# A residual block on one core: the gate and up products as one block of 1024 columns, with seven tile products in place of eight for half of the k-tiles

## The chip, the core and the metric

The kernel runs on one core of one Trainium2 chip. The metric is device time in microseconds (us) from the first to the last instruction with what lies around them; lower is better. TensorE (PE in the profile) multiplies a stationary block by a moving block, loads the stationary block with an instruction of its own (PEld), and writes sums into eight banks of PSUM, each 128 x 512 float32. VectorE (DVE) and ScalarE (ACT) read PSUM and work on tiles in SBUF. GpSimd (POOL) and SyncE (SP) mostly start transfers here. Each engine takes its instructions in the order written for it and waits at the head of its queue until what the instruction needs is there.

## The reference

One layer of a hybrid block on 256 tokens of width 2048: sparse attention and a state-space mixer in parallel, gated and projected, then a channel mixer and a final norm. The change is in the channel mixer and in what feeds it:

```python
h = h + hybrid_mixer(u, ...)                  # its last product is merged @ w_out
u2 = rms_norm(h, g_ffn[i])
gate, up = jnp.split(u2 @ w_ffn_in[i], 2, axis=-1)      # 2048 -> 2 x 5632
h = h + (jax.nn.silu(gate) * up) @ w_ffn_out[i]         # 5632 -> 2048
return rms_norm(h, g_final)
```

All of it is float32.

## The kernel before, in words

The 256 tokens are two token tiles (t = 0, 1) of 128. The width 2048 is 16 k-tiles of 128. A product of float32 operands is made from three products of a reduced float32 format: every operand is split into a high part `hi` and a rest `lo`, and the kernel adds hi x hi, hi x lo and lo x hi (L149 to L151). So one tile product (128 tokens x 128 k x 512 columns) is three TensorE instructions, and its two operands have to be split first.

For the weights this happens as they arrive. `gemm` (L140) loads four k-tiles of one block of 512 columns as one transfer of 1 MB into `raw` (three buffers), and splits them in two halves of 128 x 1024: ScalarE writes `hi` (L181), VectorE `lo` (L182). `hi` and `lo` have four buffers each, and a buffer is free again once the last product that reads it is done. A half serves 2 k-tiles x 2 token tiles x 3 = 12 products.

The channel mixer takes 512 gate columns and the 512 up columns that belong to them as one of 11 pairs (`pair`, L696). Before: one `gemm` of 16 k-tiles for gate (96 products), one for up (96), silu on ScalarE (L700), one product of the two on VectorE (L703), then eight transposes on TensorE (L212) and the split into `act` (L199, L200). After five pairs the first half of the down projection follows (`w_f2`, L717), then six more pairs and the second half.

The stationary operand is h, transposed and scaled by the gain, as `h_hi` and `h_lo`, made by `trans_split` (L205) after each of the four blocks of the output projection `w_o` (L671 to L684). The products of PSUM have four banks (`mm`), transposes two, the rest two.

The order on each engine's queue is set when the program is built, by a scheduler with priorities; loads and splits of weights carry a high one (`tc.high_priority(PRE)`). The chip only follows that order.

## Time and profile before

| what | value |
|---|---|
| median of 3 runs | 1996.29 us (1995.64 to 2485.34) |
| span of the profiled execution | 1993.2 us |
| median less span | 3.1 us |
| TensorE | 1981.7 us busy (99%), 9230 products and transposes |
| VectorE | 1247.3 us busy (63%) |
| ScalarE | 979.0 us busy (49%) |
| read from HBM | 372.02 MB, 188 GB/s over the span |

The profile's page gives for the profiled execution its span, 1993.2 us, and no time of its own; the runs' median lies 3.1 us above it, and that is the part around the span that is used below. A TensorE row's duration covers the whole pipeline, so consecutive rows overlap; what a product costs is the distance between two starts. "idle before, releaser" in a row says how long the engine had been idle ahead of the instruction and what ended that.

### The profile page before, as it was taken

The page shows a single profiled execution, that of the slowest core. Times are in us where ns is not written, and L with a number is a line of the kernel's source. Part 1 is how long each engine was busy: PE and PEld are TensorE (multiplying, and loading weights), DVE is VectorE, ACT ScalarE, POOL GpSimd, SP SyncE. Part 2 cuts the span into 40 slices and gives each one's busy share as a digit, 9 for nine tenths or more (in the row PEclk, how much of TensorE's full clock was granted, in tenths as well). Part 3 has the DMA queues.
Part 4 walks back from the last instruction along what each step waited for, and adds up shares of the span by engine and source line. Part 5 has one row for each costly group of instructions (what it writes and reads, how often), then busy time and mean ns, then how long its engine had stood idle before and what let it go on. Part 6 is the DMA issues. An engine that isn't in the chain of part 4 may idle for free.

```text
span 1993.2 us, 23301 instructions
## 1 busy us (share of the span) xinstructions
PE 1981.7 (99%) x9230; PEld 1644.7 (83%) x9230; DVE 1247.3 (63%) x1665; ACT 979.0 (49%) x1161; POOL 37.0 (2%) x87
## 2 busy tenths in 40 slices
...
GB/s 279 225 162 177 190 190 169 203 198 174 191 206 169 181 163 204 170 169 169 190 172 197 181 200 201 190 190 190 180 193 197 211 190 191 190 189 191 189 192 127
DMA packets 54429, 375.69 MB, mean 188 GB/s; under 512 B 6304, under 2 KB 6816, under 8 KB 10672
## 3 DMA queue, kind: packets, MB, share of 16 engines
...
HBM read 372.02 MB, written 2.16 MB: 188 GB/s over the span
## 4 chain that ended last, share of the span: by engine, by line
PE 98%; issue 1%; DMA 0%; DVE 0%; SPq 0%; ACT 0%; POOLq 0%; POOL 0%; DVEq 0%; ACTq 0%
PE mm L149 31%; PE mm L151 31%; PE mm L150 31%; PE yp L501 1%; PE tr L212 1%; PE tr L415 1%; PE lg L603 1%; PE tr L524 0%; PE tr L478 0%; DMA raw<-in_w_a_dram 0%; PE tr L626 0%; PE tr L569 0%; PE tr L456 0%; PE sd L391 0%; PE sd L393 0%
## 5 line engine op out<-in xcount | busy, mean ns | idle before, releaser
L182 DVE TENSOR_TENSOR lo<-raw,hi 128x1024 fp32r<-128x1024 f32 (+2 forms) x689 | 834.7, 1213 | 641.4 <-ACT hi L181 638.4
L181 ACT ACTIVATE hi<-raw 128x1024 fp32r<-128x1024 f32 (+2 forms) x689 | 723.7, 1052 | 884.0 <-PE mm L151 818.6
L150 PE MATMUL mm<-lo,uh 128*128 128x512 f32 (+2 forms) x1184 | 461.0, 389 | 0.0
L151 PE MATMUL mm<-hi,ul 128*128 128x512 f32 (+2 forms) x1184 | 458.2, 388 | 0.2 <-DVE ul L203 0.2
L149 PE MATMUL mm<-hi,uh 128*128 128x512 f32 (+2 forms) x1184 | 452.9, 389 | 1.2 <-ACT hi L181 1.2
L149 PE MATMUL mm<-hi,hh 128*128 128x512 f32 x704 | 274.8, 390 | 0.0
L151 PE MATMUL mm<-hi,hl 128*128 128x512 f32 x704 | 274.7, 390 | 0.0
L150 PE MATMUL mm<-lo,hh 128*128 128x512 f32 x704 | 274.0, 389 | 0.0
L149 PEld LDWEIGHTS mm<-hi,uh 128*128 128x128 f32 x1184 | 222.3, 188 | 44.9 <-ACT hi L181 2.1
L151 PEld LDWEIGHTS mm<-hi,ul 128*128 128x128 f32 x1184 | 222.6, 188 | 42.4 <-DVE ul L203 0.5
L150 PEld LDWEIGHTS mm<-lo,uh 128*128 128x128 f32 x1184 | 222.7, 188 | 41.3 <-DVE lo L182 0.4
L150 PEld LDWEIGHTS mm<-lo,hh 128*128 128x128 f32 x704 | 132.2, 188 | 27.2
L151 PEld LDWEIGHTS mm<-hi,hl 128*128 128x128 f32 x704 | 132.2, 188 | 27.1
L149 PEld LDWEIGHTS mm<-hi,hh 128*128 128x128 f32 x704 | 132.2, 188 | 26.7
L149 PE MATMUL mm<-hi,act 128*128 128x512 f32 x352 | 137.1, 390 | 0.0
L151 PE MATMUL mm<-hi,act 128*128 128x512 f32 x352 | 137.1, 390 | 0.0
L150 PE MATMUL mm<-lo,act 128*128 128x512 f32 x352 | 136.9, 389 | 0.0
L151 PE MATMUL mm<-hi,yl 128*128 128x512 f32 x256 | 100.4, 392 | 0.0
L150 PE MATMUL mm<-lo,yh 128*128 128x512 f32 x256 | 100.4, 392 | 0.0
L149 PE MATMUL mm<-hi,yh 128*128 128x512 f32 x256 | 100.2, 395 | 0.0
L149 PEld LDWEIGHTS mm<-hi,act 128*128 128x128 f32 x352 | 66.1, 188 | 13.7
L150 PEld LDWEIGHTS mm<-lo,act 128*128 128x128 f32 x352 | 66.1, 188 | 13.6
...
## 6 DMA issues: line engine op xcount, KB each, us to landing
raw<-in_w_f_dram SPq DMA_DIRECT2D x132, 1024.0 KB, 4.8
raw<-in_w_m_dram SPq DMA_DIRECT2D x104, 1024.0 KB, 4.8
raw<-in_w_sb_dram SPq DMA_DIRECT2D x32, 1024.0 KB, 4.8
raw<-in_w_g_dram SPq DMA_DIRECT2D x32, 1024.0 KB, 4.8
raw<-in_w_ab_dram SPq DMA_DIRECT2D x16, 1024.0 KB, 4.8
raw<-in_w_o_dram SPq DMA_DIRECT2D x16, 1024.0 KB, 4.8
abc<-acum_d POOLq DMA_DIRECT2D x8, 1024.0 KB, 5.0
...
```

What stands on the lines that cost most here:

```text
L149: nc.tensor.matmul(o, lh, rh, start=(kt == 0), stop=False)
L150: nc.tensor.matmul(o, lh, rl, start=False, stop=False)
L151: nc.tensor.matmul(o, ll, rh, start=False, stop=(kt == nk - 1))
L181: hi_ops.append(nc.scalar.activation(hi[:, o], src[:, o], AF.Copy))
L182: nc.vector.tensor_tensor(lo[:, o], src[:, o], hi[:, o].bitcast(F32), ALU.subtract)
L212: nc.tensor.transpose(tp[:, c, t * P : (t + 1) * P], src(t, o), ident)
L415: nc.tensor.transpose(tp[:, c, t * P : (t + 1) * P], xk[:, t, o : o + P], ident)
L501: nc.tensor.matmul(yp[64 * c : 64 * c + 64, m, k * P :], xdt[:, k, h * 64 : (h + 1) * 64], E[:, hh, lo : lo + n], start=(k == 0), stop=(k ...
L603: nc.tensor.matmul(lg[:, c, :n], qT[:, 2 * hp + c, t * P : (t + 1) * P], kTt[:, j, :n], start=True, stop=True)
```

## The change

`block7` takes the place of the two `gemm` calls of a pair. It keeps gate and up side by side as a block of 1024 columns and holds seven PSUM banks (p1 to p7) at once, of 128 x 512 each. The 16 k-tiles are four quads of four. In each quad, part 1 (the last two k-tiles) is done with 2 x 2 x 2 = 8 tile products as ever. Part 0 (the first two) is a 2 x 2 by 2 x 2 block product (token tiles by k-tiles, k-tiles by gate/up), done with seven tile products by the Strassen-Winograd scheme: some operands are sums and differences of blocks, and the results are put together from p1 to p7.

For the weights, VectorE makes those sums from each part 0 (`ta` at L780, 128 x 1024; `tb` at L781 and L782, two of 128 x 512) and all of it is split. Per quad the split tiles are, in order: `b` (two weight tiles), `tb`, `ta`, `b3` (one weight tile, 128 x 512), and for part 1 two halves that are called c01 and c23 here. The buffers stay three for `raw`, four for `hi` and four for `lo`. For the tokens, `quad_ops` replaces `trans_split` after each block of the output projection: it makes the sums once per quad and splits them (`opa`, `opb`, `opx`). After the last product of a pair, seven additions on VectorE (L810) and two products (L822, L823) take the place of L703. For the mixer PSUM is laid out anew: seven banks for products and one for transposes. The weights are packed in the host's layout so that a part is one transfer of 1 MB, as many as before.

```diff
-    mm = ctx.enter_context(tc.tile_pool(name="mm", bufs=4, space=bass.MemoryType.PSUM))
-    trp = ctx.enter_context(tc.tile_pool(name="trp", bufs=2, space=bass.MemoryType.PSUM))
+    mm = pctx.enter_context(tc.tile_pool(name="mm", bufs=4, space=bass.MemoryType.PSUM))
+    trp = pctx.enter_context(tc.tile_pool(name="trp", bufs=2, space=bass.MemoryType.PSUM))
...
+    def quad_ops(q):
+        f = big_t([P, 16, P], name="opf")
...
+                nc.scalar.activation(
+                    f[:, 2 * k : 2 * k + 2, :], tp[:, c, :].rearrange("p (t n) -> p t n", t=T), AF.Copy, scale=ccol(C_GF, 4 * q + k)
+                )
...
+        if QUADS[q]:
+            nc.vector.tensor_tensor(f[:, 8, :], f[:, 1, :], f[:, 3, :], ALU.add)
+            sub(f[:, 9, :], f[:, 8, :], f[:, 0, :])
+            sub(f[:, 1, :], f[:, 0, :], f[:, 1, :])
+            sub(f[:, 12, :], f[:, 2, :], f[:, 9, :])
+            sub(f[:, 10:12, :], pairs[:, 2:4, 0, :], pairs[:, 2:4, 1, :])
...
+        split(a[:, 0], a[:, 1], f[:, 0:8, :])
+        split(b[:, 0], b[:, 1], f[:, 8:12, :])
+        if QUADS[q]:
+            split(ext[:, q, 0, :], ext[:, q, 1, :], f[:, 12, :])
...
-        i, o = divmod(4 * nb, 8)
-        trans_split(
...
+        ops.append(quad_ops(nb))
...
+    pctx.close()
+    mm = ctx.enter_context(tc.tile_pool(name="mmf", bufs=7, space=bass.MemoryType.PSUM, reuse_waits="tile"))
+    trp = ctx.enter_context(tc.tile_pool(name="trf", bufs=1, space=bass.MemoryType.PSUM, reuse_waits="tile"))
...
+                    if seven and part == 0:
+
+                        b = halves(raw, ((0, 2),))
+                        ta = mid_t([P, 2, 512], name="ta")
+                        tb = mid_t([P, 2, 512], name="tb")
+                        nc.vector.tensor_tensor(ta, raw[:, 2:4, :], raw[:, 1:3, :], ALU.subtract)
+                        nc.vector.tensor_tensor(tb[:, 0, :], raw[:, 3, :], ta[:, 0, :], ALU.subtract)
+                        nc.vector.tensor_tensor(tb[:, 1, :], raw[:, 0, :], tb[:, 0, :], ALU.subtract)
+                        tbs = halves(tb, ((0, 2),))
+                        tas = halves(ta, ((0, 2),))
+                        b.update(halves(raw, ((3, 1),)))
+                    else:
+                        b = halves(raw, ((0, 2), (2, 2)))
+                if seven and part == 0:
+                    prod(1, get(q, 0), b[1])
+                    prod(2, get(q, 2), b[0])
+                    prod(6, get(q, 9), tbs[0])
+                    prod(4, get(q, 3), tbs[1])
+                    prod(7, get(q, 1), tas[1])
+                    prod(5, get(q, 8), tas[0])
+                    prod(3, get(q, 12), b[3])
...
     def pair(p):
-        ps = gemm(w_f1, 8 * p, 512, KT, lhs_h)
-        sg = ev_t([P, T, 512], "sgf")
...
+        with tc.high_priority(2 * PRE):
+            nc.scalar.activation(x1, ps[1], AF.Copy)
+            add(x2, 6, x1)
+            add(x3, 7, x2)
+            add(x1, 2, x1)
+            nc.scalar.activation(x1, x1, AF.Silu, scale=r0)
+            add(x4, 4, x3)
+            nc.scalar.activation(x4, x4, AF.Silu, scale=r1)
+            add(x2, 5, x2)
+            add(x3, 5, x3)
+            add(x2, 3, x2)
+            nc.vector.scalar_tensor_tensor(x2, x2, r0, x1, ALU.mult, ALU.mult)
+            nc.vector.scalar_tensor_tensor(x3, x3, r1, x4, ALU.mult, ALU.mult)
```

How this moves instructions shows at three places. The first is VectorE's queue in the middle of a pair. Before, it holds only `lo` splits, two for each `raw`:

```order
L182 TENSOR_TENSOR lo_10717<-raw_10714,hi_10716 128x1024
L182 TENSOR_TENSOR lo_10733<-raw_10714,hi_10732 128x1024
L182 TENSOR_TENSOR lo_10751<-raw_10748,hi_10750 128x1024
L182 TENSOR_TENSOR lo_10767<-raw_10748,hi_10766 128x1024
```

With the change, VectorE's queue for one quad in the middle of the third pair (`ta` and `tb` are those of the quad after; 10866, 10870 are ta and b3 of the quad that TensorE is at; 10897 and 10901 are c01 and c23; 10931 and 10940 are b and tb of the next quad):

```order
L747 TENSOR_TENSOR lo_10866<-ta_10856,hi_10865 128x1024
L780 TENSOR_TENSOR ta_10934<-raw_10928 128x1024
L747 TENSOR_TENSOR lo_10870<-raw_10850,hi_10869 128x512
L781 TENSOR_TENSOR tb_10935<-raw_10928,ta_10934 128x512
L747 TENSOR_TENSOR lo_10897<-raw_10894,hi_10896 128x1024
L782 TENSOR_TENSOR tb_10935<-raw_10928,tb_10935 128x512
L747 TENSOR_TENSOR lo_10901<-raw_10894,hi_10900 128x1024
L747 TENSOR_TENSOR lo_10931<-raw_10928,hi_10930 128x1024
L747 TENSOR_TENSOR lo_10940<-tb_10935,hi_10939 128x1024
L747 TENSOR_TENSOR lo_10944<-ta_10934,hi_10943 128x1024
```

Nine instructions stand where four stood for the same four k-tiles of gate and up, and the sums for a quad stand ahead of the splits of the quad before it.

The second place is the step from the output projection to the first pair, on TensorE's queue. Before, the transposes of h (`tr`) stand among the products of the first gate block, for which the other operands are ready:

```order
L151 MATMUL mm_9945<-hi_9965,hl_9275 128x512
L212 MATMUL tr_9912<-kc,h_9271 128x128
L212 MATMUL tr_9921<-kc,h_9271 128x128
L149 MATMUL mm_9946<-hi_9965,hh_9273 128x512
L212 MATMUL tr_9912<-kc,h_9272 128x128
L212 MATMUL tr_9912<-kc,h_9271 128x128
L212 MATMUL tr_9912<-kc,h_9272 128x128
L212 MATMUL tr_9921<-kc,h_9272 128x128
L212 MATMUL tr_9921<-kc,h_9271 128x128
L212 MATMUL tr_9921<-kc,h_9272 128x128
L150 MATMUL mm_9946<-lo_9966,hh_9273 128x512
```

With the change the last transposes are followed by six products p1 and p2 on the split of `b` (hi_9993), and then by products on the split of `tb` (hi_10002):

```order
L678 MATMUL tr_9947<-kc,h_9272 128x128
L678 MATMUL tr_9947<-kc,h_9271 128x128
L678 MATMUL tr_9947<-kc,h_9272 128x128
L768 MATMUL p_1713_10014<-hi_9993,opa_9440 128x512
L768 MATMUL p_1713_10014<-lo_9994,opa_9440 128x512
L768 MATMUL p_1713_10014<-hi_9993,opa_9440 128x512
L768 MATMUL p_1714_10018<-hi_9993,opa_9440 128x512
L768 MATMUL p_1714_10018<-lo_9994,opa_9440 128x512
L768 MATMUL p_1714_10018<-hi_9993,opa_9440 128x512
L768 MATMUL p_1715_10022<-hi_10002,opb_9441 128x512
L768 MATMUL p_1716_10026<-hi_10002,opa_9440 128x512
```

VectorE's queue in the same place (after the two additions that make h): the sums for the tokens of the last quad (`opf`), `ta`, the row factor, the splits `opa` and `opb` of the last quad, and only then `tb` in two steps:

```order
L687 TENSOR_TENSOR opf_9939<-opf_9939 128x128
L684 TENSOR_TENSOR opf_9939<-opf_9939 128x128 x2
L684 TENSOR_TENSOR opf_9939<-opf_9939 128x256
L684 TENSOR_TENSOR opf_9939<-opf_9939 128x128
L780 TENSOR_TENSOR ta_9997<-raw_9991 128x1024
L729 COPY rstd_9969<-rs_1699_9972 128x2
L203 TENSOR_TENSOR opa_9959<-opf_9939,opa_9959 128x1024
L203 TENSOR_TENSOR opb_9960<-opf_9939,opb_9960 128x512
L781 TENSOR_TENSOR tb_9998<-raw_9991,ta_9997 128x512
L780 TENSOR_TENSOR ta_10082<-raw_10076 128x1024
L203 TENSOR_TENSOR opx_9273<-opf_9939,opx_9273 128x128
L782 TENSOR_TENSOR tb_9998<-raw_9991,tb_9998 128x512
```

The product on hi_10002 needs both steps of `tb`; ahead of the second step there now stand the operands of the last quad and the `ta` of the quad after.

The third place is VectorE's queue at the end of a pair (p_... are the seven banks of the pair that ends, lo, ta and tb belong to the quads that follow):

```order
L810 TENSOR_TENSOR xa_11006<-p_1867_10718,xa_11006 128x512
L781 TENSOR_TENSOR tb_11042<-raw_11035,ta_11041 128x512
L747 TENSOR_TENSOR lo_10975<-raw_10972,hi_10974 128x1024
L810 TENSOR_TENSOR xb_11007<-p_1869_10726,xa_11006 128x512
L747 TENSOR_TENSOR lo_10979<-raw_10972,hi_10978 128x1024
L782 TENSOR_TENSOR tb_11042<-raw_11035,tb_11042 128x512
L747 TENSOR_TENSOR lo_11038<-raw_11035,hi_11037 128x1024
L747 TENSOR_TENSOR lo_11047<-tb_11042,hi_11046 128x1024
L810 TENSOR_TENSOR xa_11006<-p_1866_10714,xa_11006 128x512
L810 TENSOR_TENSOR xb_11007<-p_1868_10722,xb_11007 128x512
L747 TENSOR_TENSOR lo_11051<-ta_11041,hi_11050 128x1024
L810 TENSOR_TENSOR xa_11006<-p_1870_10730,xa_11006 128x512
```

The additions of a pair that ends stand among the weight splits of the first quad of the next.

## Rows read from the trace of the kernel before

**Rows 1.** The page: span, busy time of each engine, chain that ended last.

```profile
span 1993.2 us, 23301 instructions
PE 1981.7 (99%) x9230; PEld 1644.7 (83%) x9230; DVE 1247.3 (63%) x1665; ACT 979.0 (49%) x1161; POOL 37.0 (2%) x87
...
PE 98%; issue 1%; DMA 0%; DVE 0%; SPq 0%; ACT 0%; POOLq 0%; POOL 0%; DVEq 0%; ACTq 0%
```

**Rows 2.** The page, costliest groups (count, busy, mean ns) and transfers (us to landing).

```profile
L182 DVE TENSOR_TENSOR lo<-raw,hi 128x1024 fp32r<-128x1024 f32 (+2 forms) x689 | 834.7, 1213 | 641.4 <-ACT hi L181 638.4
...
raw<-in_w_f_dram SPq DMA_DIRECT2D x132, 1024.0 KB, 4.8
```

**Rows 3.** Windows in the channel mixer: busy us and count of each engine.

```profile
core 0: us, PE busy (x) PEld busy (x) DVE busy (x) ACT busy (x) POOL busy (x), PEclk, DMA share, GB/s
1299.50:1344.00 44.50, 44.50 (x202) 36.85 (x202) 22.29 (x21) 19.20 (x20) 0.00 (x0) 1.00 0.54 190
```

**Rows 4.** Timeline (start us, us) of TensorE in a pair: thirteen consecutive products, three shown.

```profile
1300.24 0.39 PE L149 MATMUL mm<-hi,hh 128*128 128x512 f32 x1
...
1302.06 0.39 PE L151 MATMUL mm<-hi,hl 128*128 128x512 f32 x1
...
1302.96 0.39 PE L149 MATMUL mm<-hi,hh 128*128 128x512 f32 x1
```

**Rows 5.** Timeline of VectorE in the channel mixer.

```profile
1299.28 1.40 DVE L703 SCALAR_TENSOR_TENSOR sgf<-mm,rstd,sgf 128x512 f32<-128x512 f32 x2
...
1303.58 1.23 DVE L182 TENSOR_TENSOR lo<-raw,hi 128x1024 fp32r<-128x1024 f32 x1 [1.49 <-ACT hi L181]
1306.17 1.29 DVE L200 TENSOR_TENSOR act<-tr,act 128x512 fp32r<-128x512 f32 x2 [1.37 <-ACT act L199]
...
1343.70 1.40 DVE L703 SCALAR_TENSOR_TENSOR sgf<-mm,rstd,sgf 128x512 f32<-128x512 f32 x2
```

**Rows 6.** Timeline of VectorE in the state-space stage, where its instructions stand back to back.

```profile
308.15 0.29 DVE L459 TENSOR_TENSOR cbm<-tr,kc 128x128 f32<-128x128 f32 x1 [1.05 <-PE tr L457]
...
313.40 1.22 DVE L182 TENSOR_TENSOR lo<-raw,hi 128x1024 fp32r<-128x1024 f32 x1
314.53 1.40 DVE L548 SCALAR_TENSOR_TENSOR acc<-mm,rsg,acc 128x512 f32<-128x512 f32 x2
315.85 0.47 DVE L422 SCALAR_TENSOR_TENSOR xsc<-tr,colp,xsc 128x255 f32<-128x255 f32 x1
```

**Rows 7.** Timeline of ScalarE in the channel mixer.

```profile
1302.48 1.06 ACT L181 ACTIVATE hi<-raw 128x1024 fp32r<-128x1024 f32 x1 [1.66 <-PE mm L151]
1305.54 1.09 ACT L199 ACTIVATE act<-tr 128x512 fp32r<-128x512 f32 x2 [1.99 <-PE tr L212]
```

**Rows 8.** Timeline of VectorE from the output projection to the channel mixer.

```profile
1254.85 1.28 DVE L678 TENSOR_TENSOR h<-mm,xr 128x512 f32<-128x512 f32 x2
...
1257.66 0.16 DVE L686 TENSOR_REDUCE ssq_h<-sq_h 128x2 f32<-128x8 f32 x1
...
1261.07 0.17 DVE L688 COPY rstd<-rs 128x2 f32<-128x2 f32 x1 [0.65 <-POOL rs L137]
```

**Rows 9.** Timeline of ScalarE in the same place.

```profile
1256.92 0.62 ACT L679 ACTIVATE xr<-h 128x512 f32<-128x512 f32 x1
...
1260.88 0.84 ACT L202 ACTIVATE hh<-tr,colp 128x256 fp32r<-128x256 f32 x2 [1.72 <-PE tr L212]
```

**Rows 10.** Timeline of TensorE at the start of the program.

```profile
7.61 0.54 PE L151 MATMUL mm<-hi,ul 128*128 128x400 f32 x1
7.94 0.54 PE L150 MATMUL mm<-lo,uh 128*128 128x400 f32 x1
...
8.95 0.34 PE L150 MATMUL mm<-lo,uh 128*128 128x400 f32 x1
9.13 0.34 PE L151 MATMUL mm<-hi,ul 128*128 128x400 f32 x1
```

More of the change, by code (lines that the diff above doesn't have):

```diff
@@ L36 @@
 SPLIT_PAIRS = 5
+QUADS = (1, 1, 1, 1)
 C_GM = 0
@@ L663, in hybrid_block, with get @@
         mT.append(m)
+    def quad_ops(q):
+        f = big_t([P, 16, P], name="opf")
+        for h in range(2):
+            tp = tr_t([P, 2, S])
+            for c in range(2):
+                for t in range(T):
+                    o = (4 * q + 2 * h + c) * P
+                    nc.tensor.transpose(tp[:, c, t * P : (t + 1) * P], h_sb[t][:, o : o + P], ident)
+            for c in range(2):
+                k = 2 * h + c
+                nc.scalar.activation(
+                    f[:, 2 * k : 2 * k + 2, :], tp[:, c, :].rearrange("p (t n) -> p t n", t=T), AF.Copy, scale=ccol(C_GF, 4 * q + k)
+                )
+        sub = lambda o, a, b: nc.vector.tensor_tensor(o, a, b, ALU.subtract)
+        pairs = f[:, 0:8, :].rearrange("p (k t) n -> p k t n", t=T)
+        if QUADS[q]:
[5 more added lines that the diff above has]
+        else:
+            sub(f[:, 8:12, :], pairs[:, :, 0, :], pairs[:, :, 1, :])
+        a = big_t([P, 2, 8, P], F32R, name="opa")
+        b = mid_t([P, 2, 4, P], F32R, name="opb")
+        split(a[:, 0], a[:, 1], f[:, 0:8, :])
+        split(b[:, 0], b[:, 1], f[:, 8:12, :])
+        if QUADS[q]:
+            split(ext[:, q, 0, :], ext[:, q, 1, :], f[:, 12, :])
+        def get(i):
+            if i < 8:
+                return a[:, 0, i, :], a[:, 1, i, :]
+            if i < 12:
+                return b[:, 0, i - 8, :], b[:, 1, i - 8, :]
+            return ext[:, q, 0, :], ext[:, q, 1, :]
+        return get
     lhs_m = lhs_quads(mT)
     h_sb = [big_t([P, D], name="h") for _ in range(T)]
-    h_hi = [big_t([P, 8, S], F32R, name="hh") for _ in range(2)]
-    h_lo = [big_t([P, 8, S], F32R, name="hl") for _ in range(2)]
+    ops = []
+    ext = mid_t([P, 4, 2, P], F32R, name="opx")
     sq4 = sm.tile([P, T, 4], F32, tag="sq4", name="sq4_h")
@@ new lines, in block7, with prod @@
+    def block7(w, first, quads, get):
+        n7 = sum(quads)
+        n1 = 4 * len(quads) - 2 * n7
+        left = {i: 3 * n7 for i in (1, 6, 7)}
+        left.update({i: 3 * (n7 + n1) for i in (2, 3, 4, 5)})
+        ps = {}
+        def prod(i, a, b):
+            start = i not in ps
+            if start:
+                ps[i] = mm.tile([P, 512], F32, tag="mm", name=nm(f"p{i}"))
+            for j, (x, y) in enumerate(((a[0], b[0]), (a[0], b[1]), (a[1], b[0]))):
+                left[i] -= 1
+                nc.tensor.matmul(ps[i], x, y, start=start and j == 0, stop=left[i] == 0)
+        for q, seven in enumerate(quads):
+            for part in range(2):
+                with tc.high_priority(PRE):
+                    raw = wraw.tile([P, 4, 512], F32, tag="raw", name=nm("raw"))
+                    nc.sync.dma_start(raw.rearrange("p k n -> p (k n)"), w[first + 2 * q + part])
+                    if seven and part == 0:
[8 more added lines that the diff above has]
+                        b.update(halves(raw, ((3, 1),)))
+                    else:
+                        b = halves(raw, ((0, 2), (2, 2)))
[7 more added lines that the diff above has]
+                    prod(3, get(q, 12), b[3])
+                else:
+                    k0 = 4 if seven else 4 * part
+                    d0 = 10 if seven else 8 + 2 * part
+                    for i, slot, n in ((2, lambda k: k0 + 2 * k, 0), (4, lambda k: k0 + 2 * k + 1, 0),
+                                       (5, lambda k: k0 + 2 * k + 1, 1), (3, lambda k: d0 + k, 1)):
+                        for k in range(2):
+                            prod(i, get(q, slot(k)), b[2 * k + n])
+        return ps
@@ L704, in pair @@
         a = big_t([P, 2, 4, S], F32R, name="act")
-        trans_split(lambda t, o: sg[:, t, o : o + P], a[:, 0], a[:, 1])
+        trans_split(lambda t, o: (x2, x3)[t][:, o : o + P], a[:, 0], a[:, 1])
         return a
```

37 lines of the change are left out of this document (26 added, 11 removed).

## The prediction

> **What bounds the kernel now.** I read the page first: TensorE is busy for 99% of the span and the chain that ended last is 98% TensorE [rows 1]. One window in the channel mixer then shows where the others stand: TensorE fills all 44.50 us at a granted clock of 1.00 (its level of 2.4 GHz), VectorE works 22.29 and ScalarE 19.20 of them [rows 3]. So a product less is worth its distance to the next start, as long as VectorE keeps up. Twelve starts lie between 1300.24 and 1302.96 [rows 4]: 2.72 / 12 = 0.2267 us a product. The same row of two pairs, at 1299.28 and 1343.70, gives 44.42 us for a pair [rows 5]; 192 products are 43.52 of it, eight transposes the other 0.90 (0.11 each). VectorE's wait ahead of each `lo` (1.49 us) is ended by ScalarE's `hi` [rows 5], and ScalarE's (1.66 us) by a product that frees the buffer [rows 7]: both have time to spare, and the buffers pace them.
>
> **What the change removes.** Of 48 products in a quad 3 go: 12 of 192 in a pair, 132 in 11 pairs, 132 x 0.2267 = 29.9 us, 1.5% of the run. It is the ceiling. A quad becomes 45 x 0.2267 = 10.2 us of TensorE, a pair 40.8 + 0.9 = 41.7. Transfers stay 88 of 1 MB.
>
> **What it adds on VectorE.** A split of 128 x 1024 takes 1.23 us, two of 128 x 512 out of PSUM 1.29 together, so 0.68 each and 0.61 from start to start [rows 5]. Back to back the next instruction starts 1.13 us after a 128 x 1024 split (313.40 to 314.53) and the two with a row factor take 1.32 (314.53 to 315.85), 0.66 each [rows 6]. A quad has six instructions of 128 x 1024 (`ta`, five splits) and three of 128 x 512 (two `tb`, `b3`): 6 x 1.13 + 3 x 0.61 = 8.6 us. The end of a pair has seven additions, two products with a row factor and two splits: 9 x 0.61 + 2 x 0.66 = 6.8. A pair is 4 x 8.6 + 6.8 = 41.3 us, against 22.29 before and against TensorE's 41.7. VectorE's spare time, which hid all splits, is gone; what comes late next is `lo`. ScalarE has 5 x 1.06 + 0.6 = 5.9 us a quad [rows 7] and stays hidden.
>
> [...]
>
> **How that meets the buffers, within a pair.** In a quad without an end of pair VectorE can run ahead only until `hi` has a free buffer for c01; that is the one of `b`, whose last product stands 27 places behind the first on the previous quad's `lo` of c01. From that start: 27 x 0.2267 = 6.1, to the release 0.42 (1302.06 to 1302.48, rows of the product and of the `hi` that it frees) [rows 4, 7], `hi` 1.06, 0.04, `lo` 1.23, 0.04 [rows 5, 7]: 8.9 us, where TensorE needs 10.2. So these quads run at TensorE's pace and VectorE is some 1.2 us ahead.
>
> **Where a pair ends.** Between the `lo` of c01 in a pair's last quad and that in the next pair's second quad VectorE's queue holds 18 weight instructions (2 x 8.6 = 17.2), six additions, two products and one split (7 x 0.61 + 2 x 0.66 = 5.6): 22.8 us. At its head it also waits, for a bank or a `hi`, about 0.3, and once for a transfer: `ta` stands early, and its `raw` can only be fetched once the split of c23 has released the buffer; 4.8 us to landing [rows 2] against 3.5 us of instructions between, 1.3. Sum 24.4. TensorE needs 90 x 0.2267 + 0.9 = 21.3. With 1.2 ahead it stands still for 24.4 - 21.3 - 1.2 = 1.9 us; without the wait for `raw` for 0.6. I take 1.7, nearer the row of the transfer. It happens in nine pairs (two end in the down projection, where VectorE has room): 15.3 us, bounds 5 and 27.
>
> **The step into the first pair.** Before, the last transposes stood among products that had their operands; the wait for h was hidden. Now, counted from the last product of the output projection: its release 0.42, h on VectorE 0.68, transposes from 1.14 to 1.7 where TensorE had work before (0.9 lost); six products on `b` until 3.2; then `tb`. ScalarE squares h until 1.9 (0.62 and 0.19 each), copies four blocks until 3.6 (two take 0.84) [rows 9]. VectorE's sums of 128 x 128 (0.29 each [rows 6]) end at 4.3, `ta` at 5.4; the row factor comes from GpSimd 3.25 us after the sum of squares ends (1257.82 to 1261.07) [rows 8], at 5.4 too; then `opa` 1.13, `opb` 0.61, first `tb` 0.61, the next quad's `ta` 1.13, `opx` 0.25, second `tb` 0.69: 9.9. `hi` of it is there at 11.0. TensorE waits 3.2 to 11.0, and 0.6 more for the next `hi`: 8.4 + 0.9 = 9.3 us, once. Lowest 4 (if the row factor and `opa` come sooner), highest 13, if its clock falls in the gap: at the start of the program, where TensorE had been waiting too, products of 400 columns start 0.33 us apart (1.2 GHz) and later 0.18 [rows 10]; with 512 columns that is 0.2 us more for each of the some 20 products until the sums have caught up, 4 us.
>
> The Trainium skill (TensorE: Matmul & The Clock Gate, "Loop structure matters more than you think") says that an idle TensorE goes back to its lower clock. No row of the mixer shows such a gap yet; by the page the highest value above would be the likelier one, and the sum 3 to 4 us more.
>
> **Small parts.** In the other three blocks of the output projection the token sums and splits add about 2 us to a VectorE that is idle 1.49 of each 2.72 us: nothing; if that cover failed, 3 x 2 = 6. Where the down projection meets a pair, two banks are still being read (two additions, 1.29): 2 us in all, bounds 0 and 5.
>
> **Sum.** -29.9 + 15.3 + 9.3 + 2 = -3.3 us on a span of 1993.2, 1989.9; with the 3.1 us between span and median, 1993 us: no change. Its own range: 1980 to 2005. Faster or slower by 2% (40 us) is about what a measurement of this kernel tells from no change.
>
> **Rivals.** *VectorE hides after all* (0.28): the scheduler's order lets TensorE use `hi` before `lo`, so an end of a pair costs 0 to 0.6; then -29.9 + 3 + 9 = -18, 1978 us, and at the ceiling 1966. For it: the steady quads' 1.2 us ahead. Against it: 41.3 of 41.7 us leaves nothing for waits at the head of a queue. *VectorE becomes the bound* (0.21): its instructions mostly wait for a semaphore of ScalarE, TensorE or VectorE itself and lose the overlap. At whole durations (1.23, 0.68, 0.74 for the row factor) a quad is 9.4 and the end of a pair 7.6, so 45.3 us a pair, and 1.6 of waits: 46.9 against 44.42, 11 x 2.5 = 27 slower, with the step and the edges 39: 2035 us. It decides from 43.4 us a pair on, where the 11.3 us paid once are no longer earned (44.42 - 11.3 / 11). Against it: the split at 313.40 needs ScalarE's `hi` like every split, and what follows still starts 1.13 us after it [rows 6]. *It doesn't do what it says* (0.01): the program holds 1980 products of the mixer's first part, 11 x 180, against 2112, so only a longer product could undo it; 0.2267 kept, nothing remains of this.
>
> **Numbers.** Forecast 0.50, the rivals 0.28, 0.21 and 0.01. The range takes in the first rival down to 1969 and the lower part of the second, up to 2024. Faster by over 2% would need more than the ceiling: 0.01. Slower by over 2% is the upper half of the second rival: 0.10. Within 2%: 0.89.
>
> **What would show it.** In the profile after: 9098 products and transposes; 45 products of a middle quad in 10.2 us with no idle TensorE; VectorE near 41 us busy a pair, at 95% of the window; TensorE idle for 1 to 2 us in the first quads of a pair, ended by VectorE's `lo`; one gap of about 8 us ended by ScalarE's `hi` of `tb`, with the clock still 1.00. I am wrong if a pair takes over 45 us, if the middle quads wait, or if `hi` rather than `lo` ends the waits.

## The result and the profile after

The changed kernel takes **2010.43 us** (median of four runs, 2009.86 to 2013.1) against 1995.97 before: a ratio of 1.0077 with an interval of 1.0065 to 1.0090. It is slower by 0.8%, with 132 products less. The profiled execution has a span of 2008.6 us against 1993.2, 15.4 more.

The page of the changed kernel, which answers to [rows 1]:

```profile
span 2008.6 us, 23561 instructions
...
PE 1969.9 (98%) x9098; PEld 1620.3 (81%) x9098; DVE 1467.9 (73%) x1978; ACT 1058.2 (53%) x1272; POOL 37.0 (2%) x87
...
PE 81%; DVE 10%; DMA 6%; issue 2%; ACT 1%; POOL 0%; SPq 0%; DVEq 0%; POOLq 0%; ACTq 0%
```

9098 products and transposes are there, 132 fewer. But the chain of waits, 98% TensorE before, now goes for 10% through VectorE and for 6% through transfers. This share says where to look and not how much is lost: 17% of the span would be some 340 us, while the span grew by 15.4 with products worth 29.9 taken out, so some 45 us are lost in all.

Four stretches at the step into the first pair in the same view as [rows 3], then two in the middle of the mixer:

```profile
core 0: us, PE busy (x) PEld busy (x) DVE busy (x) ACT busy (x) POOL busy (x), PEclk, DMA share, GB/s
1256.00:1260.00 4.00, 2.25 (x12) 1.66 (x12) 2.61 (x8) 3.78 (x10) 2.51 (x5) 1.00 0.00 0
1260.00:1264.00 4.00, 0.00 (x0) 0.00 (x0) 3.64 (x6) 0.32 (x2) 0.36 (x2) 0.78 0.00 0
1264.00:1268.00 4.00, 1.94 (x4) 1.33 (x5) 2.88 (x5) 3.04 (x4) 0.00 (x0) 0.50 0.00 0
1268.00:1272.00 4.00, 4.00 (x17) 3.22 (x16) 4.00 (x6) 2.22 (x3) 0.00 (x0) 0.86 0.32 80
1388.00:1432.00 44.00, 42.63 (x188) 34.03 (x187) 41.32 (x48) 25.81 (x29) 0.00 (x0) 1.00 0.55 189
1376.00:1400.00 24.00, 24.00 (x107) 19.89 (x106) 22.43 (x26) 14.47 (x17) 0.00 (x0) 1.00 0.61 214
```

In the last two quads of the third pair (1376 to 1400) TensorE is never idle. Over a whole pair (1388 to 1432) it is, though VectorE works 41.32 of 44 us as forecast, 94%. And at the step the granted clock falls to 0.50, the level of 1.2 GHz, after a gap.

TensorE's timeline at the step and at one end of a pair (start, us; in brackets the idle time and what ended it):

```profile
1258.03 0.39 PE L768 MATMUL p<-hi,opa 128*128 128x512 f32 x1
1266.06 0.80 PE L768 MATMUL p<-hi,opb 128*128 128x512 f32 x1 [7.65 <-ACT hi L746]
...
1267.61 0.63 PE L768 MATMUL p<-hi,opb 128*128 128x512 f32 x1
1268.03 0.63 PE L768 MATMUL p<-lo,opb 128*128 128x512 f32 x1
...
1401.37 1.14 PE L768 MATMUL p<-hi,opa 128*128 128x512 f32 x3
1403.51 0.50 PE L768 MATMUL p<-hi,opb 128*128 128x512 f32 x1 [1.01 <-DVE xb L810]
...
1413.53 0.50 PE L768 MATMUL p<-lo,opb 128*128 128x512 f32 x1 [0.34 <-DVE lo L747]
```

There is one gap of 7.65 us, ended by ScalarE's `hi` of `tb`. Behind it starts are 0.42 us apart instead of the 0.2267 of [rows 4] until the clock is back: some eight products, 1.6 us. The third wait is the one I had not seen: the product of `opb` into p5 waits for an addition, `xb` (line 810). It is there in each of the nine pairs that take in the end of the pair before. Together with the two slightly late products just ahead of it, it costs 1.00 to 1.92 us beyond a normal start, 13.2 us in all. Next to it stand the waits for a `lo` in a pair's second quad, 0.2 to 2.4 us, 7.3 in all, and waits for a `lo` in the third quad of three pairs (6, 8 and 10), 3.9.

VectorE in front of that product, with the next `ta` a quad later:

```profile
1400.44 0.68 DVE L810 TENSOR_TENSOR xa<-p,xa 128x512 f32<-128x512 f32 x1
1401.04 0.68 DVE L747 TENSOR_TENSOR lo<-raw,hi 128x512 fp32r<-128x512 f32 x1
1401.64 1.22 DVE L780 TENSOR_TENSOR ta<-raw 128x1024 f32<-128x1024 f32 x1
1402.78 0.68 DVE L810 TENSOR_TENSOR xb<-p,xb 128x512 f32<-128x512 f32 x1
...
1411.12 1.23 DVE L780 TENSOR_TENSOR ta<-raw 128x1024 f32<-128x1024 f32 x1 [1.13 <-DMA raw<-in_w_f_dram]
```

p5 is read by two additions (1400.44 and 1402.78). Seven sums fill seven banks, so the next pair's p5 needs the bank of this one, and a split and a `ta` stand between the two additions. The last row shows VectorE itself standing still, for a transfer. Grouped by line over the mixer, 1280 to 1880 (busy, mean ns | idle time before them, and what ended it):

```profile
L747 DVE TENSOR_TENSOR lo<-ta,hi 128x1024 fp32r<-128x1024 f32 x42 | 51.2, 1219 | 10.3 <-ACT hi L746 10.2
L747 DVE TENSOR_TENSOR lo<-tb,hi 128x1024 fp32r<-128x1024 f32 x42 | 51.1, 1218 | 2.2 <-ACT hi L746 1.5
L780 DVE TENSOR_TENSOR ta<-raw 128x1024 f32<-128x1024 f32 x41 | 50.1, 1222 | 31.2 <-DMA raw<-in_w_f_dram 31.1
```

The engine that had 41.3 us of work for 41.7 us of TensorE's time was idle 31 us in front of `ta` and 10 in front of a `lo`. Where in a pair that was shows from one `lo` of c01 to the next, the instruction from which and to which the prediction counts. First the third and fourth pair, then the eighth:

```profile
1392.21 1.22 DVE L747 TENSOR_TENSOR lo<-raw,hi 128x1024 fp32r<-128x1024 f32 x1
...
1416.34 2.35 DVE L747 TENSOR_TENSOR lo<-raw,hi 128x1024 fp32r<-128x1024 f32 x2
...
1436.40 1.22 DVE L747 TENSOR_TENSOR lo<-raw,hi 128x1024 fp32r<-128x1024 f32 x1
...
1702.25 2.35 DVE L747 TENSOR_TENSOR lo<-raw,hi 128x1024 fp32r<-128x1024 f32 x2
...
1711.75 1.22 DVE L780 TENSOR_TENSOR ta<-raw 128x1024 f32<-128x1024 f32 x1 [2.54 <-DMA raw<-in_w_f_dram]
1712.89 0.68 DVE L747 TENSOR_TENSOR lo<-raw,hi 128x512 fp32r<-128x512 f32 x1
...
1724.82 1.22 DVE L747 TENSOR_TENSOR lo<-raw,hi 128x1024 fp32r<-128x1024 f32 x1
```

```profile
1713.63 0.50 PE L768 MATMUL p<-lo,opx 128*128 128x512 f32 x1 [0.51 <-DVE lo L747]
```

The rows at 1392.21, 1436.40 and 1724.82 are c01 of a pair's last quad, those at 1416.34 and 1702.25 (c01 and c23 in one row) c01 of a second quad. The end of a pair, last quad to second quad, took 24.13 us here (1392.21 to 1416.34), and 24.0 to 25.4 over the nine ends: 24.5 in the mean, 1.65 of it idle. The middle, second quad to last quad, took 20.06 us here and 20.1 to 24.3 over the nine pairs in front of these ends: 21.3 in the mean, 2.6 of it idle. In the eighth pair it was 22.57. There `ta` waited 2.54 us for its transfer, the split of b3 behind it was late, and TensorE waited for that split (1713.63). A pair took 44.2 to 47.0 us instead of 44.43 before.

### The profile page after: what moved, and what is told of

It reads as the page before. It is cut to its first block, busy times and chain, and to the rows that moved or that the text cites. A ratio compares the mean times of both kernels' runs of the same rounds, so it can differ in the third digit from the quotient of the medians.

```text
span 2008.6 us, 23561 instructions
## 1 busy us (share of the span) xinstructions
PE 1969.9 (98%) x9098; PEld 1620.3 (81%) x9098; DVE 1467.9 (73%) x1978; ACT 1058.2 (53%) x1272; POOL 37.0 (2%) x87
## 4 chain that ended last, share of the span: by engine, by line
PE 81%; DVE 10%; DMA 6%; issue 2%; ACT 1%; POOL 0%; SPq 0%; DVEq 0%; POOLq 0%; ACTq 0%
PE mm L152 23%; PE mm L154 23%; PE mm L153 23%; PE p L768 8%; DVE lo L747 5%; DMA raw<-in_w_f_dram 5%; DVE ta L780 2%; PE yp L504 1%; DVE xa L810 1%; DVE xb L810 1%; ACT hi L746 1%; DVE tb L781 1%; PE tr L418 1%; PE lg L606 1%; DVE tb L782 0%
## 5 line engine op out<-in xcount | busy, mean ns | idle before, releaser
L185 DVE TENSOR_TENSOR lo<-raw,hi 128x1024 fp32r<-128x1024 f32 (+2 forms) x513 | 618.5, 1208 | 387.9 <-ACT hi L184 386.4
L184 ACT ACTIVATE hi<-raw 128x1024 fp32r<-128x1024 f32 (+2 forms) x513 | 536.9, 1049 | 624.8 <-PE mm L154 560.3
L768 PE MATMUL p<-hi,opa 128*128 128x512 f32 x880 | 301.4, 394 | 0.1
L746 ACT ACTIVATE hi<-raw 128x1024 fp32r<-128x1024 f32 (+1 forms) x176 | 164.7, 950 | 91.0 <-PE p L768 82.2
L768 PEld LDWEIGHTS p<-hi,opa 128*128 128x128 f32 x880 | 166.0, 189 | 37.6 <-ACT hi L746 3.7
L747 DVE TENSOR_TENSOR lo<-raw,hi 128x1024 fp32r<-128x1024 f32 (+1 forms) x176 | 187.6, 1083 | 4.8 <-ACT hi L746 4.3
L768 PE MATMUL p<-lo,opa 128*128 128x512 f32 x440 | 174.6, 397 | 2.4 <-DVE lo L747 2.2
L768 PE MATMUL p<-hi,opb 128*128 128x512 f32 x352 | 131.2, 397 | 17.4 <-DVE xb L810 9.8
L768 PEld LDWEIGHTS p<-lo,opa 128*128 128x128 f32 x440 | 83.2, 189 | 24.5 <-DVE lo L747 8.0
L768 PEld LDWEIGHTS p<-hi,opb 128*128 128x128 f32 x352 | 66.8, 190 | 34.7 <-DVE xb L810 13.7
```

The source lines that it names most:

```text
L184: hi_ops.append(nc.scalar.activation(hi[:, o], src[:, o], AF.Copy))
L185: nc.vector.tensor_tensor(lo[:, o], src[:, o], hi[:, o].bitcast(F32), ALU.subtract)
L746: nc.scalar.activation(hi, src, AF.Copy)
L747: nc.vector.tensor_tensor(lo, src, hi.bitcast(F32), ALU.subtract)
L768: nc.tensor.matmul(ps[i], x, y, start=start and j == 0, stop=left[i] == 0)
```

## The experiments

Each version was timed beside the kernel before. "A pair" is the distance of the same VectorE row of two neighbouring pairs in the middle of the mixer.

| run | us | ratio to before | a pair, us |
|---|---|---|---|
| the change | 2010.4 | 1.0077 [1.0065, 1.0090] | 44.2 to 47.0 |
| e1: p5 copied out | 2006.6 | 1.0051 [1.0037, 1.0065] | 44.4 to 47.8 |
| e2: `ta` late | 2009.3 | 1.0070 [1.0058, 1.0083] | 45.3 to 46.8 |
| e3: first quad with eight | 1976.2 | 0.9903 [0.9890, 0.9917] | 42.47 |
| e4: gap filled | 2007.4 | 1.0063 [1.0050, 1.0075] | 44.5 to 47.4 |
| e5: `ta` on GpSimd | 2035.5 | 1.0202 [1.0189, 1.0216] | 47.6 to 49.5 |
| e6: `ta`, `tb` on GpSimd | 2042.7 | 1.0238 [1.0224, 1.0252] | 47.9 to 48.5 |
| e7: last quad with eight | 1994.9 | 0.9997 [0.9989, 1.0006] | 43.2 to 44.8 |
| e8: eight everywhere | 1996.8 | 1.0007 [0.9998, 1.0016] | 44.47 |
| e9: `ta` late, `tb` first | 1996.8 | 1.0006 [0.9998, 1.0015] | 43.87 |
| e10: step written early | 2000.7 | 1.0025 [1.0016, 1.0035] | 44.4 to 47.2 |
| e11: e9 and e10 | 1987.2 | 0.9958 [0.9945, 0.9970] | 43.87 |
| e12: e11 and e1 | 1987.1 | 0.9958 [0.9945, 0.9970] | 43.88 |
| e13: without `ta` | 1979.0 | 0.9918 [0.9904, 0.9931] | 42.26 |
| e14: e8, `ta` on GpSimd | 1997.2 | 1.0010 [1.0001, 1.0019] | 44.47 |
| e15: e11 without `ta` | 1973.8 | 0.9892 [0.9878, 0.9905] | 42.27 |
| e16: e3 and e9 | 1974.6 | 0.9896 [0.9881, 0.9911] | 42.47 |

**The bank (e1).** My first theory was the wait that the trace showed most plainly.

```
-            add(x2, 5, x2)
-            add(x3, 5, x3)
+            x5 = sm.tile([P, 512], F32, tag="rtmp", name=nm("x5"))
+            nc.scalar.activation(x5, ps[5], AF.Copy)
+            nc.vector.tensor_tensor(x2, x5, x2, ALU.add)
+            nc.vector.tensor_tensor(x3, x5, x3, ALU.add)
```

> ScalarE copies p5 into an SBUF tile at the end of a pair and VectorE's two additions of p5 read the copy, so p5's bank comes free without VectorE's queue. In the changed kernel TensorE waits once a pair (nine times, 1.0 to 1.9 us, 13.2 us in all) for VectorE's second addition of p5. Theory A (the bank's waits are a cost of their own): they vanish, nothing takes their place, about 1998 us. Theory B (VectorE as a whole is late by that much, whichever of its instructions TensorE meets first): the waits come back as waits for a `lo` in the first two quads of a pair, with the same sum, 2007 to 2011 us. Theory C (VectorE loses its time where `ta` waits for its transfer): the transfers don't come earlier, so as B.

It took 2006.6 us, 0.4 below B's range and 8.6 above A's; its five runs spread from 2002.4 to 2008.3. No product waits for an addition any more; TensorE at the same place in a later pair:

```profile
1449.23 0.39 PE L768 MATMUL p<-hi,opb 128*128 128x512 f32 x1
1450.33 0.50 PE L768 MATMUL p<-lo,opa 128*128 128x512 f32 x1 [0.71 <-DVE lo L747]
...
1451.36 0.85 PE L768 MATMUL p<-hi,opa 128*128 128x512 f32 x3
1452.66 0.50 PE L768 MATMUL p<-hi,opa 128*128 128x512 f32 x1 [0.46 <-ACT hi L746]
```

Waits for a `lo` and for a `hi` have taken the place of the bank's. The wait with the largest label was only where TensorE met a late VectorE first: theory A fell.

**The transfer (e2).** The same sums; only where `ta` stands on VectorE.

```
+  with tc.issue_after(c01s[-1].ins):     # lo of c01 of the quad before
       nc.vector.tensor_tensor(ta, raw[:, 2:4, :], raw[:, 1:3, :], ALU.subtract)
```

> `ta` of a quad is put on VectorE's queue behind the split of c01 of the quad before it, instead of anywhere the scheduler likes (often ahead of that split, and ahead of the addition that frees p5's bank). Nothing is added or taken away. In the changed kernel VectorE stands idle 32.0 us of the mixer in `ta`, for its transfer. Theory A (bank): the addition of p5 is no longer behind a `ta`, so most of the 13.2 us of bank waits go and the waits for a `lo` stay: 1999 us. Theory B (VectorE's total): VectorE works as much as before and the sum of TensorE's waits hardly moves: 2006 to 2011 us. Theory C (the transfer at the head of VectorE's queue): VectorE's 32 us of idle time fall below 10, its instructions come earlier, and the bank waits and the waits for a `lo` (11 us) both go: 1984 to 1990 us.

2009.3 us: no theory but B has the time, and yet C's first half came true. VectorE by line:

```profile
L749 DVE TENSOR_TENSOR lo<-tb,hi 128x1024 fp32r<-128x1024 f32 x42 | 51.5, 1225 | 40.2 <-ACT hi L748 40.2
L784 DVE TENSOR_TENSOR ta<-raw 128x1024 f32<-128x1024 f32 x42 | 51.3, 1222 | 0.8 <-DMA raw<-in_w_f_dram 0.8
```

The wait for the transfer went from 31 to 1 us, and 40 us in front of the split of `tb` came up. VectorE makes the last `tb`, ScalarE needs 1.06 us for its `hi`, and VectorE's queue holds nothing between that `tb` and the `lo` that needs it. The idle time changed its place, not its size: from 1316 to 1492 VectorE works 160.61 of 176 us, in the change 161.05.

**How much VectorE has to do, and where (e3, e7, e8).** One line of the change decides which quads of a pair have seven products. (e8 also leaves out the additions at the end of a pair that only the seven need.)

```
-QUADS = (1, 1, 1, 1)
+QUADS = (0, 1, 1, 1)     # e3;  e7: (1, 1, 1, 0);  e8: (0, 0, 0, 0)
```

> The first quad of every pair has eight products a k-tile pair of groups (as the last two k-tiles of each quad have) instead of seven, the other three keep seven: 33 products more in the 11 pairs' first quads, 99 instead of 132 saved (22.4 us instead of 29.9), and VectorE has `ta`, two `tb` and two splits less in the quad on which the end of the pair before lands (some 4 us less a pair). The step into the first pair needs no weight sums. Theory A (bank): the addition that frees a bank is still in VectorE's queue among the splits, half of the 13.2 us stays; step 8.5 to 3: 1996.3 - 22.4 + 6.6 + 3 + 4 (waits for `lo`) = 1988 us. Theory B (VectorE's total): some 4 us of room a pair end nearly all waits, 1996.3 - 22.4 + 3 + 2 = 1979 us. Theory C (transfer): three `ta` a pair still wait, 1985 us.

> The same work as in the version whose first quad has eight products (99 products saved, VectorE 37.1 us a pair), but the quad with eight is the last of each pair, not the first, on which the end of the pair before lands. If only VectorE's total a pair counts: 1976 us and the step into the first pair, 10, so 1986 us. If VectorE cannot carry its spare time over (the buffers let it run ahead by a microsecond only), the waits at the end of a pair stay, 9 x 2.2: 1996.3 - 22.4 + 10 + 20 + 2 = 2006 us.

> The block of 1024 columns alone: eight products in all quads, nothing saved, no sums of weights; what is left of the change is token-major order, four token differences a quad, four banks instead of seven for a pair, one bank for transposes and one addition at the end of a pair. VectorE works about 23 us a pair. If the price of the change lies in the sums for the seven products: 1996 to 1998 us, no waits in the middle. If it lies in the block's form (one bank for transposes, the step): 2003 us or more.

e3 came out at 1976.2, 3 us below the lowest forecast, B's 1979. The same 176 us of e3, then of e7 (pairs of the first half, and some of the down projection behind them):

```profile
1316.00:1492.00 176.00, 176.00 (x794) 145.46 (x793) 151.72 (x168) 99.24 (x110) 0.00 (x0) 1.00 0.58 206
```

```profile
1316.00:1492.00 176.00, 173.73 (x775) 141.99 (x775) 148.78 (x164) 95.51 (x108) 0.00 (x0) 1.00 0.57 200
```

With the light quad first, where the end of the pair before lands, TensorE is not idle in this stretch; a pair is 42.47, which is the 44.47 of e8 less nine products. e8 says that the block with its single transpose bank costs nothing that can be measured once the sums for the seven are gone. The same amount of work with the light quad last (e7) takes 1994.9, between the two forecasts: 8 us are its step into the first pair, some 2 the clock behind it, and the rest 0.7 to 2.4 us more a pair. So VectorE's room counts where the extra work lands; it cannot all be carried over.

**The clock (e4).**

```
+  for _ in range(32):     # behind the second product of the first pair, in order
+      last = nc.tensor.matmul(warm, wz[:, :P], wz, start=True, stop=True).ins
```

> 32 products of zeros (bf16, 128x512, into the transposes' bank, read by nobody) fill TensorE's gap of 7.65 us at the step into the first pair; everything else keeps its place. In the changed kernel the granted clock falls to 0.50 there and the products behind the gap start 0.42 us apart for some eight of them (about 1.6 us). If an idle TensorE is what lowers the clock: the granted clock stays at 1.00, the first products behind the gap start 0.23 us apart, and the kernel takes 1.6 us less, 2008.8 us. If the products in the gap push the first `tb` product out (they take 32 x 0.213 = 6.8 us), no gain: 2010.4.

```profile
1260.00:1264.00 4.00, 4.00 (x20) 1.83 (x19) 3.64 (x6) 0.59 (x2) 0.64 (x2) 1.00 0.00 0
1264.00:1268.00 4.00, 3.05 (x13) 1.44 (x12) 2.88 (x5) 2.77 (x4) 0.00 (x0) 1.00 0.00 0
1268.00:1272.00 4.00, 4.00 (x20) 3.28 (x19) 4.00 (x6) 3.10 (x4) 0.00 (x0) 1.00 0.21 41
```

The clock stays at 1.00, so it was the empty TensorE that lowered it. The time is 2007.4, in the direction forecast, but the intervals of the two ratios overlap: 1.6 us is read from the rows, not from this time.

**Less work on VectorE through GpSimd (e5, e6, e14).**

```
-  nc.vector.tensor_tensor(ta, raw[:, 2:4, :], raw[:, 1:3, :], ALU.subtract)
+  nc.gpsimd.tensor_tensor(ta, raw[:, 2:4, :], raw[:, 1:3, :], ALU.subtract)
```

> All quads keep seven products a pair (132 saved), but `ta` (one 128x1024 difference a quad) is computed by GpSimd, so VectorE has 4 x 1.13 = 4.5 us less a pair (36.8 instead of 41.3 against TensorE's 41.7). Theory B (VectorE's total at the end of a pair): nearly all waits in the middle of the mixer go, the step into the first pair (8.5) and its clock (1.6) stay: 1996.3 - 29.9 + 10 + 2 = 1978 us. Theory L (where an engine has little room, the order and the hand-overs between ScalarE, VectorE and TensorE cost, not the work): `ta` must now come from a third engine, so the waits stay and change their names, 2003 to 2012 us. If GpSimd and VectorE slow each other, VectorE's 128x1024 split takes longer than 1.23 us in the trace and the gain is smaller by that, about 1990 us.

> As the run before, and the two `tb` (128x512 each) are on GpSimd too: VectorE has 4.9 us less again, 31.9 us a pair. Theory B: nothing more to win in the middle; at the step into the first pair `tb` no longer stands behind the sums of the last token tiles, so its 8.5 us shrink to 4 or 5: 1973 us. If GpSimd's chain of three (ta, tb, tb) is longer than the 10.2 us of a quad, GpSimd is the bound: above 1996 us.

2035.5 and 2042.7. For e5 all three forecasts were too low by 23 us or more. e6 is above 1996 us, as its second forecast said, but not for that reason: GpSimd's three instructions take 2.71, 1.99 and 2.05 us in the mean, 6.8 of a quad's 10.2. GpSimd and VectorE in e5:

```profile
1302.76 2.69 POOL L780 TENSOR_TENSOR ta<-raw 128x1024 f32<-128x1024 f32 x1 [9.09 <-DMA raw<-in_w_f_dram]
1314.53 2.37 POOL L780 TENSOR_TENSOR ta<-raw 128x1024 f32<-128x1024 f32 x1 [9.07 <-DMA raw<-in_w_f_dram]
```

```profile
1303.94 0.69 DVE L810 TENSOR_TENSOR xa<-p,xa 128x512 f32<-128x512 f32 x1 [0.75 <-PE p L768]
...
1314.18 0.68 DVE L810 TENSOR_TENSOR xa<-p,xa 128x512 f32<-128x512 f32 x1
1314.78 2.67 DVE L747 TENSOR_TENSOR lo<-raw,hi 128x512 fp32r<-128x512 f32 x1
```

A split of 0.69 us that begins while GpSimd works (1314.53 to 1316.90) takes 2.67 us: it ends 0.55 after GpSimd. The 42 splits of this shape from 1280 to 1880 take 1932 ns in the mean instead of 683. That is 52 us lost on VectorE, where 42 `ta` taken off it at 1.13 us save 47; and `tb` waits for a slower `ta` on top, 30.6 us. The addition at 1303.94, with one operand in PSUM, lies inside another `ta` of GpSimd (1302.76 to 1305.45) and keeps its 0.69. The Trainium skill (GPSIMD Engine Reference, "Key points") says that GpSimd shares its SBUF interfaces with VectorE and that they contend when VectorE's instruction has two SBUF inputs; the trace agrees, with 2.67 against 0.69 us. To see it alone, e14 puts the same GpSimd work where VectorE is idle half the time.

> The block with eight products everywhere (nothing saved, VectorE half idle), and on GpSimd one 128x1024 difference a quad that nobody reads. If GpSimd and VectorE hold each other up: VectorE's instructions that meet GpSimd's last longer in the trace (the shape with 0.68 us up to 2 us or more), GpSimd's last 2.4 to 2.8 us and VectorE's spare time hides it, 1997 to 2000 us. If they don't: VectorE's durations stay at 1.22 and 0.68 us, 1996.8 us, and the slowness of the GpSimd versions is of another kind.

```profile
1311.48 2.40 POOL L790 TENSOR_TENSOR ta<-raw 128x1024 f32<-128x1024 f32 x1 [10.06 <-DMA raw<-in_w_f_dram]
1321.03 3.15 POOL L790 TENSOR_TENSOR ta<-raw 128x1024 f32<-128x1024 f32 x1 [7.15 <-DMA raw<-in_w_f_dram]
```

```profile
1319.56 2.36 DVE L747 TENSOR_TENSOR lo<-raw,hi 128x1024 fp32r<-128x1024 f32 x2 [2.09 <-ACT hi L746]
```

1997.2 us: it is hidden. Here it is GpSimd that stretches: 2.40 us alone, 3.15 where its first 0.89 us meet VectorE's splits. VectorE's split of 128x1024 keeps 1228 ns against 1221 in e8, so the forecast of longer VectorE instructions did not show in the mean. Only three splits began behind a GpSimd difference, and these took 1.33 to 3.38 us. The time itself decides nothing: 1997.2 fits both forecasts.

**Order alone (e9 to e12).** From e2 followed a version that fills VectorE's 1 us.

```
   ta (late, as in e2), tb, tb
+  with tc.issue_after(tb1.ins):
       lo of b          # now between the last tb and the lo of tb
```

> On top of the run that put `ta` late: both `tb` stand ahead of the split of `b` in VectorE's queue, so that VectorE splits `b` (1.2 us) while ScalarE makes the `hi` of `tb` (1.06 us). In that earlier run VectorE's wait for the transfer fell from 31 to 1 us, but 40 us of waiting for the `hi` of `tb` came in its place, 0.96 us a quad; nothing but order is changed here. Theory B1 (VectorE's work alone, 41.3 us a pair plus the end of a pair, is too much): the waits come back elsewhere, 2003 to 2010 us. Theory B2 (VectorE's work just fits, its idle time behind other engines, some 4.3 us a pair, is what is too much): VectorE's idle time in front of `lo` of `tb` falls below 10 us and nothing takes its place, a pair takes 42 to 43 us instead of 44.2 to 46.6: 1988 to 1995 us.

1996.8 us, 13.7 less than the change: 1.8 above B2's range and 6 below B1's. VectorE by line:

```profile
L750 DVE TENSOR_TENSOR lo<-tb,hi 128x1024 fp32r<-128x1024 f32 x42 | 51.3, 1222 | 3.7 <-ACT hi L748 1.5
...
L784 DVE TENSOR_TENSOR ta<-raw 128x1024 f32<-128x1024 f32 x42 | 51.1, 1217 | 0.8 <-DMA raw<-in_w_f_dram 0.8
L818 DVE TENSOR_TENSOR xa<-p,xa 128x512 f32<-128x512 f32 x44 | 30.1, 683 | 12.9 <-PE p L771 12.9
```

Both waits are gone, and what remains is mostly VectorE waiting for TensorE's sums. Pairs settle at 43.87, above the 42 to 43 of the forecast: some 2 us a pair stay at its end. The same rows as above show why:

```profile
1389.09 0.69 DVE L818 TENSOR_TENSOR xa<-p,xa 128x512 f32<-128x512 f32 x1 [1.04 <-PE p L771]
1389.70 1.21 DVE L750 TENSOR_TENSOR lo<-raw,hi 128x1024 fp32r<-128x1024 f32 x1
...
1412.85 1.21 DVE L750 TENSOR_TENSOR lo<-raw,hi 128x1024 fp32r<-128x1024 f32 x1
```

The end of a pair now takes VectorE 23.15 us with 0.14 idle, so it is work alone, 1.85 more than the 21.3 that TensorE needs. The middle takes 20.7: VectorE does not run ahead there, because the first addition of the pair's end stands in front of the last quad's c01 and waits 1.04 us for TensorE's sum.

For the step, the first seven products' load, sums and splits are written ahead of the last additions of h:

```
   ps = gemm(w_o, 4 * nb, 512, KT, lhs_m)
+  if nb == 3:
+      pre = load_part(w_f1, 0, QUADS[0])     # raw, b, ta, tb and their splits
```

> Only the step into the first pair: the load, the sums of weights and the splits of the first seven k-tile products of the mixer are written ahead of the last additions of h, so that VectorE and ScalarE do them while TensorE ends the output projection (VectorE idles there for 5.2 us). If the step costs what the trace shows (8.5 us of waiting, 1.6 of a lower clock, nothing of it given back later): 2000 us and no wait over 1.5 us there. If VectorE is no earlier in the pairs because of it and the bank waits only start sooner: the gap goes and the first pair ends later by as much as it gains, 2006 to 2010 us.

> Both changes of order together, all 132 products saved. If the two costs add up: the time of the run with `tb` first, less 9 to 10 us; under B2 1979 to 1985 us, under B1 1993 to 2000 us.

> The run before, and p5 is copied out of its bank by ScalarE at the end of a pair. If the bank of p5 is what is left at the end of a pair once VectorE has fewer waits: 9 x 1 us less than the run before; if VectorE's lateness is what is left, no difference beyond 3 us.

e10 took 2000.7, as the first forecast said: the step costs its 10 us, and nothing is given back. e11 took 1987.2: 13.7 and 9.8 are 23.5, and 23.2 are measured, so the two costs add up. e12 is the same as e11, so p5's bank is not what is left.

**VectorE's work, taken away without another engine (e13, e15).** Both leave the difference `ta` out and take raw k-tiles for it.

```
-  ta = mid_t([P, 2, 512], name="ta")
-  nc.vector.tensor_tensor(ta, raw[:, 2:4, :], raw[:, 1:3, :], ALU.subtract)
+  ta = raw[:, 2:4, :]
```

> `ta` is left out: the raw k-tiles stand in its place in the splits and in `tb` (the mixer's sums are then other sums; the work left out is one 128x1024 difference a quad on VectorE and nothing else). All 132 products saved, order of the change, VectorE 36.8 us a pair. If VectorE's work is the cause (and GpSimd's version lost because the two engines hold each other up): nearly no waits behind the step, 1996 - 29.9 + 10 (step and clock) + 2 = 1978, up to 1985 us where the `hi` of `tb` is still waited for. If the hand-overs are the cause: the waits stay, above 1998 us.

> The better order and the step written early (1987.2 us with all the work), and `ta` left out as in the run before last: VectorE has 4.5 us a pair less. If the 2 us a pair that are left there go with VectorE's work: a pair at TensorE's 41.7 us, 1966 to 1970 us, the ceiling. If they are the hand-over at a pair's end (bank, `hi`): 1984 to 1987 us.

e13 took 1979.0, within its first forecast: with 4.5 us less on VectorE a pair the kernel takes 31 us less than the change; some 3 of them lie at the step, whose gap is 4.90 us instead of 7.65. With `ta` its wait for the transfer goes too, of which 5.9 us come back in front of `tb`, so e13 does not part work from waiting; e15 does (1973.8 against the 1987.2 of e11), where the better order is there already. A pair is 42.26, and TensorE works 175.52 of 176 us:

```profile
1316.00:1492.00 176.00, 175.52 (x787) 143.88 (x786) 149.24 (x171) 105.56 (x118) 0.00 (x0) 1.00 0.59 206
```

e15 took 1973.8, 4 us above its forecast of 1966 to 1970: a pair stays at 42.27, the same as with the worse order, with a wait of 0.16 for p5's bank in each. Where the other 0.3 to 0.4 us a pair above 41.7 go was not tried.

**The best version that computes the reference (e16).** Light first quad and better order.

> First quad of a pair with eight products, and the order with `ta` late and `tb` first. TensorE waits 0.65 us in the middle of the mixer without the order, so it can give no more than 1 us: 1975 to 1976.5 us. If the order is worth more than the trace shows (the ends of a pair): below 1974 us.

1974.6 us, 0.9896 [0.9881, 0.9911]: 20.9 us below the kernel before, of 22.4 that its 99 products are worth. It beats both kernels; against e3 the gain is 1.6 us with overlapping intervals.

## Why the prediction was wrong

The forecast was 1993, no change; measured were 2010.4, 0.8% slower with an interval clear of no change. That is above the forecast's own range of 1980 to 2005. The wide range reached 2024 only for the slower rival, whose mechanism did not come, so that it holds 2010 is luck. In the span the sum had to give +15.4 and gave -3.3.

- **The ceiling held.** 132 products at 0.2267 us are 29.9: e8's 44.47 less e3's 42.47 is 2.00 us for nine products, 0.222 each.
- **VectorE's work held.** Forecast 41.3 us a pair, 41.32 measured in a window of 44. Starts are 1.14 us (1401.64 to 1402.78) and 0.60 us apart, as in [rows 5, 6]. The Trainium skill (VectorE: DVE Perf Modes, "The DRAIN you can't avoid") has the next operation wait for the end of the pipe, which would put them 1.22 and 0.68 apart, but adds: "A next op that is not held starts earlier". The trace agrees with the addition. So the slower rival, whole durations, is not what happened, though the time lies between it and the forecast.
- **The middle quads held in part.** 24.00 of 24.00 us are busy in the third pair, but in three pairs TensorE waited 0.8 to 1.6 us in the third quad. This and the pairs of over 45 us were signs of being wrong, and both came.
- **The step held in size**: 9.3 us forecast (8.4 in the gap, 0.9 at the transposes), 8.5 measured (7.8 and 0.7 beyond normal starts), ended by the `hi` of `tb`. My sign "clock still 1.00" failed: it fell to 0.50, for 1.6 us, where the highest value had set 4. The Trainium skill (TensorE: Matmul & The Clock Gate, "Loop structure matters more than you think") has an idle TensorE going back to its lower clock, and the trace agrees.
- **The step that failed is the lead: "VectorE is some 1.2 us ahead", which "Where a pair ends" takes off in 24.4 - 21.3 - 1.2.** The 24.4 held: 24.5 measured, with 1.65 us idle where the two guesses (0.3 and 1.3) made 1.6. But to be 1.2 ahead again at each end, VectorE had to pass the two quads between in 20.4 - 1.2 = 19.2 us, and it took 21.3. It was idle there for 2.6 us: 1.6 in front of `ta`, for a transfer, and 0.9 in front of the `lo` of `ta`, for its `hi`. The prediction let `ta` wait "once", at the end of a pair, and asked in the middle only for the buffer of c01. Without a lead its own working gives 24.4 - 21.3 = 3.1 us for an end of a pair.
- **What it cost.** Measured on TensorE: 24.4 us of waits for the bank and for a `lo`, 3.2 us of lower clock behind two of them, for which the sum had nothing, and some 7 us in small pieces: 34.3 us over nine ends (the nine distances between third quads, 409.6 us, less 9 x 41.7), 3.8 each instead of my 1.7. That is 19.0 us more than forecast; the step's clock adds 1.6, the step itself was 0.8 less and the small parts some 1 less, which makes the 18.7 by which the sum was off. The sign "TensorE idle 1 to 2 us, ended by `lo`" was half right: the larger wait is ended by the addition of p5.
- **The reason behind it**: I counted VectorE's work to 0.1 us and walked its queue for waits only where a pair ends. At 41.3 of 41.7 us each hand-over in the queue (`ta` at a transfer, `lo` of a sum at its `hi`) takes from the lead, wherever in the pair it stands. e2 showed that removing one wait brings up the other, e9 that removing both gives 13.7 us back, though still no lead; e3, e13 and e15 show that with 4 us of room what is left costs 0.1 to 0.6 us a pair.
